# Trailing sums of the pooling branch on GpSimd; the subtractions stay on VectorE

## The chip, the core and the metric

The kernel runs on one core of one Trainium2 chip. The metric is the device time of one launch in microseconds (us). The kernel before took 1399.68 us in the median of 3 runs (1397.62 to 1403.03). All arithmetic is in 32-bit floats.

The engines are named as the profile names them: PE is TensorE (PEld its weight loads), DVE is VectorE, ACT is ScalarE, POOL is GpSimd, SP is SyncE. Each engine runs its own queue in program order. SP computes nothing here: it issues nearly all loads from memory, so its queue is the list of loads.

## The reference, cut to what matters

One decoder layer over 256 tokens of width 2048. A conditioning vector `c` gives shift, scale and gate vectors by a product with `w_ada` (2048 x 12288). The normed and modulated tokens go through one projection `w_in`, whose columns feed two branches: sparse attention (an indexer picks 64 keys per query) and the pooling branch. Both are joined by `w_out`; then follows a mixture of 32 experts. The pooling branch:

```python
cs = jnp.cumsum(pg, axis=1)
lag = cs_pad[:, lo, jnp.arange(POOL_GROUPS)[None, :], :]
count = jnp.minimum(t + 1, win[None, :]).astype(jnp.float32)
mixed = (cs - lag) / count[None, :, :, None] - pg
y = jnp.einsum('bsgc,gcd->bsgd', mixed.astype(p.dtype), w_pool) * pool_scale
```

There are 1024 pooling channels in 4 groups with windows 2, 4, 8 and 16: the mean over the last 2, 4, 8 or 16 tokens, minus the token itself, then one 256 x 256 matrix per group.

## The kernel before, in words

The channels lie on the 128 partitions and the 256 tokens along the free axis, so the pooled input `ppT` is 128 x 8 x 256 (two chunks of channels for each group). `pool_sums` (line 510) builds the sums by doubling: level 0 adds each token's neighbour (window 2) for all 8 chunks, level 1 adds the level before at a distance of 2 (window 4) for the last 6 chunks, then 4 and 2 chunks. The levels alternate between two buffers, `wa` and `wb`. On each level line 516 adds, line 517 copies the first tokens, which have no partner. Line 521 corrects the first 16 tokens of a group for the shorter window, and line 522 subtracts the token itself and writes back into `ppT`. `pool_map` (line 524) loads `w_pool` and does the matrices on PE (line 531).

What stands around it. The program is written against a scheduler that orders the instructions of each engine by priority and by its own estimates of time, so an edit on one engine can move instructions on all. The projection (`project`, line 458) runs in five blocks of rows of `w_in`; on the last block the indexer (line 362) and `pool_sums` come in between. PE writes projections into two PSUM banks called `mm`; line 470 on DVE adds a bank to `pidx` or `pqkv` and so frees it.

Fills: 64 slices of `w_ada` of 1 MB each (line 177 loads on SP, line 178 multiplies and adds on DVE, 128 x 2048 each) make gate 1, the second shift and scale, and gate 2. They are needed only later, and go in between other work. Their loads have three slots, first the two halves of G4 and one of G5, later G5's is replaced by B8 (shown as `w`). A slot is free for its next load when line 178 has read it. All sums go into an accumulator in G6. The last fill belongs to gate 2, which the first expert stage needs late (line 290).

After the projection: `out_proj` (line 602) for the pooling half and then for the attention half. Line 608 loads `w_out` in 16 pieces of 1 MB, line 613 is the product on PE, line 617 scales a PSUM bank by gate 1 and line 618 adds it to the residual, both on DVE. After each quarter of the attention half a routing block transposes and multiplies for the router (lines 679 to 697). The routing itself is a chain of small DVE instructions (lines 708 to 789). Then `gather` multiplies tokens into expert slots (line 796 on PE, line 800 on DVE), and the experts follow: line 815 and line 856 load 2 MB tiles of expert weights into a ring of seven 16 KB places (G5, G1, G2, G3, G0, G7, G4), line 820 and 861 multiply. Six of these loads stand in SP's queue before the number of tokens per expert is read (line 952), the seventh behind it; the seventh goes to G4, so it waits for the last fill's line 178.

In the order listings below, `g_70` is G4, `g_71` is G5 (the pooled input lies in its upper half), `g_72` is G6, and `g_68` and `g_69` are the places of `w_in` and `w_out`.

Of the kernel before, what the change touches and what calls it, by code (L numbers as in the profile page):

```python
# [16 lines left out]
P = 128  # L17
D = 2048
NT = 2
S = 256  # L20
# [27 lines left out]
EDGE = 16  # L48
# [31 lines left out]
def layer_kernel(ctx: ExitStack, tc: tile.TileContext, x, c, w_ada, b_ada, norm1_g, w_in, q_norm_g,  # L80
                 k_norm_g, w_pool, pool_scale, w_out, norm2_g, w_grp, w_exp, w1, w3, w2,
                 kconst, kband, out):
    nc = tc.nc
# [71 lines left out]
    for v, r, j, at in ((v8T, RB, 0, None), (v8T, RB, 1, 3), (v8T, RB, 2, 4), (v4T, RR, 0, None), (v4T, RR, 1, 4)):  # L155
        src = norm2_g[0] if at is None else b_ada[at * D:(at + 1) * D]
        nc.scalar.dma_start(v[:, j].rearrange("p k r -> p (k r)").rearrange("p (k r) -> p k r", r=r),
                            src.rearrange("(k p r) -> p k r", p=P, r=r))
    edge = one.tile([P, 4, EDGE], F32, name="edge")
# [104 lines left out]
    for kq in range(4):  # L264
# [5 lines left out]
        dst = hT[:, kq * 4:kq * 4 + 4]  # L270
# [239 lines left out]
    def pool_sums():  # L510
        wa = one.tile([P, 8, S], F32, tag="N0", name="wa")
        wb = one.tile([P, 8, S], F32, tag="N1", name="wb")
        src = ppT
        for lv, dst in enumerate((wa, wb, wa, wb)):
            c0, lag = 2 * lv, 1 << lv
            nc.vector.tensor_add(dst[:, c0:8, lag:S], src[:, c0:8, lag:S], src[:, c0:8, 0:S - lag])
            nc.vector.tensor_copy(dst[:, c0:8, 0:lag], src[:, c0:8, 0:lag])
            src = dst
        for g, dst in enumerate((wa, wb, wa, wb)):
            sl = slice(2 * g, 2 * g + 2)  # L520
            nc.vector.tensor_mul(dst[:, sl, 0:EDGE], dst[:, sl, 0:EDGE], edge[:, g][:, None, :].to_broadcast([P, 2, EDGE]))
            nc.vector.scalar_tensor_tensor(ppT[:, sl], dst[:, sl], 1.0 / POOL_WINDOWS[g], ppT[:, sl], op0=ALU.mult, op1=ALU.subtract)

    def pool_map():
# [14 lines left out]
    for b, (k0, nk) in enumerate(BLOCKS):  # L539
        block_scales(b)  # L540
        for k in range(k0, k0 + nk):
            h = hcols(k, slice(0, S))
            nc.scalar.activation(h, h, AF.Identity, scale=s1T[:, k:k + 1], bias=sh1T[:, k:k + 1])
        nxt = block_ada(b + 1) if b + 1 < len(BLOCKS) else []
        last = b + 1 == len(BLOCKS)
        for pi, part in enumerate(PARTS):
            if nxt:
                nxt.pop(0)()
            project(b, part)
            if pi == 2 and nxt:  # L550
                nxt.pop(0)()
            if last and part[0] == "kw":
                indexer()
                pool_sums()
            if b in FILLS:
                fill(FILLS[b][pi])
        for piece in nxt:
            piece()
# [427 lines left out]
```

## Time and profile before

| | |
|---|---|
| median of 3 runs | 1399.68 us |
| the profiled execution | 1398.5 us, span 1396.5 us |
| busy in the span: PE, DVE, ACT, POOL | 1071.1, 446.9, 100.1, 9.1 us |
| read from memory | 554.31 MB, 398 GB/s over the span |
| mean granted clock of PE | 0.888 |

The span is the stretch from the first to the last instruction of the profiled execution; 2 us lie around it. Times in a view count from the span's start. A line of a timeline has start, duration, engine, source line, operation, output and inputs, shapes, how many instructions were merged, and in brackets how long the engine was idle ahead of it and what ended that. `SPq` is SP's queue: its instructions only issue a load. The table of windows gives for each stretch how long each engine was busy, the granted clock of PE, the share of time in which the 16 DMA engines were busy, and the rate.

### The profile page before, as it was taken

How to read it: one execution, taken by the hardware profiler on the slowest of the kernel's cores; microseconds unless marked ns; L12 is line 12 of the kernel's file. 1: busy time of each engine (PE TensorE's matmuls, PEld its weight loads, DVE VectorE, ACT ScalarE, POOL GpSimd, SP SyncE). 2: the span in 40 equal slices, each digit the busy share in tenths (PEclk: the TensorE clock that was granted, in tenths of full speed). 3: DMA queues.
4: the chain of work that ended last, by engine and by line, in shares of the span. 5: the costliest groups of instructions: out<-in, count | busy, mean ns of one | idle time of the engine just before them, and what ended most of it. 6: DMA issues, size and time to landing. Idle time of an engine off the chain costs nothing.

```text
span 1396.5 us, 12529 instructions
## 1 busy us (share of the span) xinstructions
PE 1071.1 (77%) x5243; PEld 432.8 (31%) x5243; DVE 446.9 (32%) x725; ACT 100.1 (7%) x225; POOL 9.1 (1%) x11
## 2 busy tenths in 40 slices
PE   4899998998997776677758767676775867768566
PEld 2355654544456231122213213122211311312111
DVE  1196667999677210201202101020220202102002
ACT  3100000324222000000000000000000000000000
POOL 1000000000000000000000000000000000000000
PEclk9899999999997979889979988887997988898787
DMA  9999998999999799999999999999999999999997
GB/s 320 318 385 385 400 381 323 342 357 332 401 360 405 325 428 427 428 428 427 427 429 427 428 428 428 428 428 428 427 429 427 428 428 427 429 427 428 428 403 260
DMA packets 104907, 557.27 MB, mean 399 GB/s; under 512 B 18856, under 2 KB 33168, under 8 KB 72848
## 3 DMA queue, kind: packets, MB, share of 16 engines
q1 hardware_dynamic: 101312, 554.22, 97.8%
q10 hardware_dynamic: 3472, 2.20, 0.5%
q8 instruction: 43, 0.70, 0.2%
q14 instruction: 16, 0.13, 0.0%
q0 software_dynamic: 64, 0.02, 0.0%
HBM read 554.31 MB, written 2.10 MB: 398 GB/s over the span
## 4 chain that ended last, share of the span: by engine, by line
DMA 54%; PE 30%; DVE 8%; SPq 4%; issue 3%; ACT 1%; ACTq 0%; DVEq 0%
DMA w<-in_w_dram 49%; PE mm L820 10%; PE mm L613 5%; PE mm L475 5%; PE b L861 4%; DVE g L178 3%; DMA g<-in_w_ada_dram 3%; PE b L485 2%; DMA g<-in_w_in_dram 2%; SPq L876 1%; SPq L815 1%; DVE bacc L219 1%; PE b L796 1%; DVE g L408 1%; DMA v8T<-in_b_ada_dram 1%
## 5 line engine op out<-in xcount | busy, mean ns | idle before, releaser
L820 PE MATMUL mm<-w,xg 128*32 128x512 f32 x2048 | 338.0, 694 | 163.6 <-DMA w<-in_w_dram 163.6
L861 PE MATMUL b<-w,t 128*32 128x512 f32 x896 | 181.1, 697 | 86.4 <-DMA w<-in_w_dram 80.9
L820 PEld LDWEIGHTS mm<-w,xg 128*32 128x32 f32 x2048 | 76.3, 124 | 412.6 <-DMA w<-in_w_dram 231.0
L800 DVE TENSOR_SCALAR xg<-b,sc2T,sh2T 128x128 f32<-128x128 f32 x128 | 42.3, 403 | 386.4 <-PE b L796 386.4
L475 PE MATMUL mm<-g,hT 128*128 128x512 f32 (+1 forms) x320 | 127.9, 553 | 12.7 <-DMA g<-in_w_in_dram 7.8
L178 DVE SCALAR_TENSOR_TENSOR g<-g,sT,g 128x2048 f32<-128x2048 f32 x52 | 121.9, 2344 | 9.9 <-DMA g<-in_w_ada_dram 9.8
L613 PE MATMUL mm<-g,mix 128*128 128x512 f32 x256 | 114.7, 601 | 4.2 <-DVE t L617 4.2
L861 PEld LDWEIGHTS b<-w,t 128*32 128x32 f32 x896 | 42.3, 118 | 220.2 <-DMA w<-in_w_dram 118.6
L841 DVE TENSOR_TENSOR t<-b,gt 128x512 f32<-128x512 f32 (+1 forms) x33 | 20.9, 671 | 278.6 <-PE b L861 253.7
L475 PEld LDWEIGHTS mm<-g,hT 128*128 128x128 f32 x320 | 57.3, 199 | 79.1 <-issue 65.4
L613 PEld LDWEIGHTS mm<-g,mix 128*128 128x128 f32 x256 | 48.1, 193 | 60.7 <-issue 55.0
L844 PE MATMUL mm<-t,gwT 128*128 128x512 f32 (+1 forms) x132 | 63.6, 613 | 1.6 <-DVE t L841 1.1
L796 PEld LDWEIGHTS b<-gq,x1c 128*128 128x128 f32 x512 | 59.8, 196 | 13.1 <-issue 6.7
L796 PE MATMUL b<-gq,x1c 128*128 128x128 f32 x512 | 62.6, 282 | 1.2 <-DVE gq L786 1.2
L824 ACT ACTIVATE t<-mm 128x512 f32<-128x512 f32 x8 | 4.8, 597 | 816.8 <-PE mm L820 816.8
L485 PE MATMUL b<-hT,g 128*128 128x256 f32 x256 | 56.9, 380 | 0.9 <-DMA g<-in_w_in_dram 0.9
L485 PEld LDWEIGHTS b<-hT,g 128*128 128x128 f32 x256 | 48.3, 190 | 11.7 <-issue 3.3
L846 DVE TENSOR_TENSOR xs<-xs,mm 128x512 f32<-128x512 f32 (+1 forms) x66 | 44.3, 671 | 18.9 <-PE mm L844 18.7
L825 DVE TENSOR_TENSOR t<-t,mm 128x512 f32<-128x512 f32 x8 | 5.5, 688 | 117.5 <-PE mm L820 117.5
L219 DVE SCALAR_TENSOR_TENSOR bacc<-g,sT,bacc 128x1024 f32<-128x1024 f32 x28 | 35.9, 1282 | 7.6 <-DMA g<-in_w_ada_dram 5.1
L844 PEld LDWEIGHTS mm<-t,gwT 128*128 128x128 f32 x132 | 21.7, 192 | 43.5 <-DVE xs L846 28.4
L178 DVE SCALAR_TENSOR_TENSOR g<-w,sT,g 128x2048 f32<-128x2048 f32 x12 | 28.1, 2346 | 2.3 <-DMA w<-in_w_ada_dram 2.2
(208 smaller groups left out, 511.6 us busy)
## 6 DMA issues: line engine op xcount, KB each, us to landing
w<-in_w_dram SPq DMA_DIRECT2D x188, 2048.0 KB, 22.1
g<-in_w_ada_dram SPq DMA_DIRECT2D x52, 1024.0 KB, 8.2
g<-in_w_ada_dram SPq DMA_DIRECT2D x44, 512.0 KB, 9.4
g<-in_w_in_dram SPq DMA_DIRECT2D x21, 1024.0 KB, 10.3
g<-in_w_out_dram SPq DMA_DIRECT2D x16, 1024.0 KB, 9.6
w<-in_w_ada_dram SPq DMA_DIRECT2D x12, 1024.0 KB, 7.6
w<-in_w_ada_dram SPq DMA_DIRECT2D x20, 512.0 KB, 9.6
g<-in_w_in_dram SPq DMA_DIRECT2D x14, 512.0 KB, 8.7
```

What stands on the lines that cost most here:

```text
L178: nc.vector.scalar_tensor_tensor(acc, w, sT[:, k:k + 1], acc, op0=ALU.mult, op1=ALU.add)
L219: nc.vector.scalar_tensor_tensor(acc, w[:, kk], sT[:, k:k + 1], acc, op0=ALU.mult, op1=ALU.add)
L475: nc.tensor.matmul(po[:, :width], lhsT=hcols(k0 + j, slice(i * P, (i + 1) * P)), rhs=w[:, j], start=(j == 0), stop=(j == nk - 1))
L485: nc.tensor.matmul(ppool[n][:, u], lhsT=w[:, j, u * P:(u + 1) * P], rhs=hcols(k, slice(0, S)), start=(k == 0 and u % 2 == 0), stop=(k == K ...
L613: nc.tensor.matmul(po, lhsT=mix[:, k, i * P:(i + 1) * P], rhs=ws[k // 4][:, k % 4], start=(k == 0), stop=(k == 7))
L796: nc.tensor.matmul(px[:, u], lhsT=x1c[i][:, k // RB, k % RB], rhs=gq[:, i].rearrange("p e s -> p (e s)"), start=(i == 0), stop=(i == NT - 1))
L800: nc.vector.tensor_scalar(xg[:, k], px[:, u], sc2T[:, k:k + 1], sh2T[:, k:k + 1], op0=ALU.mult, op1=ALU.add)
L820: nc.tensor.matmul(h[e * CAP:(e + 1) * CAP, :], lhsT=xg[:, k, e * CAP:(e + 1) * CAP], rhs=ws[e][:, r], start=(k == 0), stop=(k == KC - 1), ...
L841: nc.vector.tensor_mul(y[:, 0:m], py, gt2[:, c0:c0 + m])
L844: nc.tensor.matmul(pz[:, 0:m], lhsT=gwT[:, i], rhs=y[:, 0:m], start=True, stop=True)
L846: nc.vector.tensor_add(xv, xv, pz[:, 0:m])
L861: nc.tensor.matmul(py[n // 2][e * CAP:(e + 1) * CAP, (n % 2) * 512:(n % 2 + 1) * 512], lhsT=aT[:, f, e * CAP:(e + 1) * CAP], rhs=ws[e][:, ...
```

## The change

The four additions, the four copies and the four corrections of the first tokens are issued on GpSimd in place of VectorE. Line 522 stays on VectorE.

```diff
@@ -513,12 +513,12 @@
         src = ppT
         for lv, dst in enumerate((wa, wb, wa, wb)):
             c0, lag = 2 * lv, 1 << lv
-            nc.vector.tensor_add(dst[:, c0:8, lag:S], src[:, c0:8, lag:S], src[:, c0:8, 0:S - lag])
-            nc.vector.tensor_copy(dst[:, c0:8, 0:lag], src[:, c0:8, 0:lag])
+            nc.gpsimd.tensor_add(dst[:, c0:8, lag:S], src[:, c0:8, lag:S], src[:, c0:8, 0:S - lag])
+            nc.gpsimd.tensor_copy(dst[:, c0:8, 0:lag], src[:, c0:8, 0:lag])
             src = dst
         for g, dst in enumerate((wa, wb, wa, wb)):
             sl = slice(2 * g, 2 * g + 2)
-            nc.vector.tensor_mul(dst[:, sl, 0:EDGE], dst[:, sl, 0:EDGE], edge[:, g][:, None, :].to_broadcast([P, 2, EDGE]))
+            nc.gpsimd.tensor_mul(dst[:, sl, 0:EDGE], dst[:, sl, 0:EDGE], edge[:, g][:, None, :].to_broadcast([P, 2, EDGE]))
             nc.vector.scalar_tensor_tensor(ppT[:, sl], dst[:, sl], 1.0 / POOL_WINDOWS[g], ppT[:, sl], op0=ALU.mult, op1=ALU.subtract)
```

GpSimd's queue gets the twelve instructions in one run, between the memset of line 366 and the third memset of line 281; the correction for a group stands right behind the copy of the level that it needs. Ahead of the first addition the build puts one instruction that reloads GpSimd's library; it waits for nothing.

DVE's queue at the pooling sums, before (`wa` and `wb` are the two buffers, `mm` a bank of the projection):

```order
L516 TENSOR_TENSOR wa<-g_71 128x8x255
L517 COPY wa<-g_71 128x8
L178 SCALAR_TENSOR_TENSOR g_72<-g_70,sT,g_72 128x2048
L516 TENSOR_TENSOR wb<-wa 128x6x254
L517 COPY wb<-wa 128x6x2
L521 TENSOR_TENSOR wa<-wa,edge 128x2x16
L470 TENSOR_TENSOR pidx<-pidx,mm 128x512
L178 SCALAR_TENSOR_TENSOR g_72<-g_70,sT,g_72 128x2048
L470 TENSOR_TENSOR pidx<-pidx,mm 128x512
L516 TENSOR_TENSOR wa<-wb 128x4x252
L517 COPY wa<-wb 128x4x4
L522 SCALAR_TENSOR_TENSOR g_71<-wa,g_71 128x512
```

The same place in the changed kernel, from the same point on:

```order
L178 SCALAR_TENSOR_TENSOR g_72<-g_70,sT,g_72 128x2048
L470 TENSOR_TENSOR pidx<-pidx,mm 128x512
L178 SCALAR_TENSOR_TENSOR g_72<-g_70,sT,g_72 128x2048
L470 TENSOR_TENSOR pidx<-pidx,mm 128x512
L178 SCALAR_TENSOR_TENSOR g_72<-g_71,sT,g_72 128x2048
L351 TENSOR_TENSOR g_73<-pidx,kc 128x64
L352 TENSOR_TENSOR g_73<-pidx,kc 128x64
L353 TENSOR_TENSOR g_73<-pidx,kc 128x64
L354 TENSOR_TENSOR g_73<-pidx,kc 128x64
L522 SCALAR_TENSOR_TENSOR g_71<-wa,g_71 128x512
L470 TENSOR_TENSOR pidx<-pidx,mm 128x512
L470 TENSOR_TENSOR pidx<-pidx,mm 128x80
```

The sums are gone, line 522 now waits for GpSimd, and the third line 470 stands behind it. Ahead of the last of the four lines 522 stand three lines 178, counted from here, where there were five.

SP's queue from the last load of `w_out` to the third load of expert weights, before:

```order
L608 DMA g_68<-in_w_out_dram 128x4x512
L177 DMA g_70<-in_w_ada_dram 128x2048
L177 DMA w<-in_w_ada_dram 128x2048
L177 DMA g_70<-in_w_ada_dram 128x2048 x2
L177 DMA w<-in_w_ada_dram 128x2048
L177 DMA g_70<-in_w_ada_dram 128x2048 x2
L177 DMA w<-in_w_ada_dram 128x2048
L815 DMA w<-in_w_dram 128x4096
```

And in the changed kernel:

```order
L608 DMA g_68<-in_w_out_dram 128x4x512
L177 DMA g_70<-in_w_ada_dram 128x2048 x2
L177 DMA w<-in_w_ada_dram 128x2048
L177 DMA g_70<-in_w_ada_dram 128x2048 x2
L177 DMA w<-in_w_ada_dram 128x2048
L177 DMA g_70<-in_w_ada_dram 128x2048 x2
L177 DMA w<-in_w_ada_dram 128x2048
L177 DMA g_70<-in_w_ada_dram 128x2048 x2
L177 DMA w<-in_w_ada_dram 128x2048
L177 DMA g_70<-in_w_ada_dram 128x2048 x2
L177 DMA w<-in_w_ada_dram 128x2048
L815 DMA w<-in_w_dram 128x4096
```

Eight fills stood there, now there are fifteen: four fewer stand ahead of the last `w_out` load (47 against 51), and three more ahead of this load of expert weights (62 against 59).

DVE's queue at the first gather, before:

```order
L786 TENSOR_SCALAR gq<-t_1899,rs_1857 128x128 x2
L789 TENSOR_TENSOR t_1899<-t_1899,cmb 128x256
L178 SCALAR_TENSOR_TENSOR g_72<-w,sT,g_72 128x2048
L178 SCALAR_TENSOR_TENSOR g_72<-g_70,sT,g_72 128x2048
L800 TENSOR_SCALAR xg<-b_1921,sc2T,sh2T 128x128 x8
L800 TENSOR_SCALAR xg<-b_1946,sc2T,sh2T 128x128 x8
L805 COPY gwT<-sm 128x256
L178 SCALAR_TENSOR_TENSOR g_72<-g_70,sT,g_72 128x2048
```

And in the changed kernel:

```order
L786 TENSOR_SCALAR gq<-t_1899,rs_1857 128x128 x2
L789 TENSOR_TENSOR t_1899<-t_1899,cmb 128x256
L178 SCALAR_TENSOR_TENSOR g_72<-g_70,sT,g_72 128x2048
L800 TENSOR_SCALAR xg<-b_1921,sc2T,sh2T 128x128 x8
L800 TENSOR_SCALAR xg<-b_1946,sc2T,sh2T 128x128 x8
L805 COPY gwT<-sm 128x256
```

The last fill moves from behind line 805 to ahead of the lines 800. In the routing ahead of this piece, the line 178 that stood between lines 731 and 732 is gone too, and the line 178 of the 63rd fill stands ahead of the last line 697.

## Rows read from the trace of the kernel before

**Rows 1.** The chain that ended last, by engine (the page, part 4).
```profile
DMA 54%; PE 30%; DVE 8%; SPq 4%; issue 3%; ACT 1%; ACTq 0%; DVEq 0%
```

**Rows 2.** Windows: start:end, length, busy us by engine, PEclk, DMA share, GB/s.
```profile
218.70:242.20 23.50, 19.89 (x63) 9.22 (x63) 23.41 (x39) 1.00 (x4) 0.00 (x0) 0.93 0.91 324
242.20:337.10 94.90, 89.01 (x329) 46.66 (x327) 91.27 (x180) 31.64 (x100) 4.11 (x3) 1.00 0.94 360
337.10:387.80 50.70, 49.95 (x133) 23.64 (x134) 38.69 (x35) 16.27 (x40) 0.00 (x0) 0.97 0.97 359
387.80:454.40 66.60, 56.94 (x263) 40.03 (x262) 50.95 (x79) 16.45 (x28) 0.00 (x0) 0.85 0.96 380
454.40:462.60 8.20, 8.20 (x79) 3.55 (x80) 7.25 (x17) 0.00 (x0) 0.00 (x0) 1.00 0.12 27
462.60:1381.00 918.40, 651.70 (x3646) 198.32 (x3636) 121.07 (x255) 8.40 (x13) 0.00 (x0) 0.86 1.01 425
```

**Rows 3.** Timeline of DVE at the pooling sums.
```profile
204.53 4.73 DVE L178 SCALAR_TENSOR_TENSOR g<-g,sT,g 128x2048 f32<-128x2048 f32 x2
218.79 2.28 DVE L516 TENSOR_TENSOR wa<-g 128x2040 f32<-128x2040 f32 x1 [9.52 <-ACT g L488]
...
233.32 0.68 DVE L470 TENSOR_TENSOR pidx<-pidx,mm 128x512 f32<-128x512 f32 x1
...
241.47 0.68 DVE L522 SCALAR_TENSOR_TENSOR g<-wb,g 128x512 f32<-128x512 f32 x1
```

**Rows 4.** Windows, line 516 alone: length, DVE busy, PEclk, DMA share, GB/s.
```profile
218.70:242.20 23.50, 5.88 (x4) 0.93 0.91 324
```

**Rows 5.** Groups of DVE instructions, 218 to 243: busy us, mean ns, idle.
```profile
L521 DVE TENSOR_TENSOR wa<-wa,edge 128x32 f32<-128x32 f32 x2 | 0.4, 180 | 0.0
...
L517 DVE COPY wb<-wa 128x12 f32<-128x12 f32 (+1 forms) x2 | 0.3, 165 | 0.0
```

**Rows 6.** Timeline of PE, 225 to 338.
```profile
225.89 4.55 PE L475 MATMUL mm<-g,hT 128*128 128x512 f32 x16
234.05 6.31 PE L475 MATMUL mm<-g,hT 128*128 128x80 f32 x16 [3.61 <-DVE pidx L470]
...
264.36 1.13 PE L531 MATMUL mm<-g,g 128*128 128x256 f32 x4
...
327.77 0.63 PE L593 MATMUL b<-kc,g 128*128 128x128 f32 x4 [1.78 <-DVE g L575]
329.07 1.13 PE L597 MATMUL sm<-spare,g 128*128 128x512 f32 x2 [0.68 <-ACT spare L594]
...
333.64 0.75 PE L307 MATMUL fl<-kc,t 128*128 128x128 f32 x4 [0.72 <-ACT t L304]
337.85 10.31 PE L613 MATMUL mm<-g,mix 128*128 128x512 f32 x20 [3.46 <-DVE t L617]
```

**Rows 7.** Timeline of SP's queue: loads issued.
```profile
384.33 3.81 SPq L608 DMA_DIRECT2D g<-in_w_out_dram  x2
...
461.13 4.73 SPq L815 DMA_DIRECT2D w<-in_w_dram  x5
```

**Rows 8.** Timeline of DVE, routing and first gather.
```profile
437.68 0.23 DVE L697 TENSOR_TENSOR lr<-lr,sm 128x72 f32<-128x72 f32 x1 [3.78 <-PE sm L686]
...
440.06 2.33 DVE L178 SCALAR_TENSOR_TENSOR g<-g,sT,g 128x2048 f32<-128x2048 f32 x1
...
452.52 2.64 DVE L800 TENSOR_SCALAR xg<-b,sc2T,sh2T 128x128 f32<-128x128 f32 x8 [0.31 <-PE b L796]
...
458.76 2.35 DVE L178 SCALAR_TENSOR_TENSOR g<-g,sT,g 128x2048 f32<-128x2048 f32 x1
```

**Rows 9.** Timeline of POOL, memsets.
```profile
174.26 0.53 POOL L366 MEMSET qiT<- 128x512 f32 x1 [140.96 <-PE sm L229]
260.41 1.82 POOL L281 MEMSET g<- 128x2048 f32 x1 [85.63 <-PE fl L290]
```

## Prediction

> **What bounds the kernel now.** I read the chain that ended last first: 54% of it is DMA and 30% PE, and only 8% is DVE [rows 1]. So an engine that gets lighter is worth nothing by itself; it has to let loads go out earlier. The table of windows says where that is possible. From 462.6 to 1381 the DMA engines are busy all the time at 425 GB/s [rows 2]: there the end follows the moment at which the stream of expert weights starts, and nothing else. Ahead of it the share is 0.91 to 0.97, with one real hole, 8.2 us at a share of 0.12 (454.4 to 462.6), ahead of the seventh load of expert weights [rows 2]. DVE is busy 23.41 of 23.50 us at the pooling sums and 91.27 of 94.90 us behind them, and PE is nearly full beside it [rows 2]. So in this part three resources are close to full together, and a gain on one soon meets the next.
>
> **What leaves DVE.** The four additions are 5.88 us [rows 4]; four corrections at 0.18 and four copies at 0.165 are 1.4 us [rows 5]. Together 7.3 us of DVE. They don't come off the time directly. The new order also lets DVE do a fill in the 9.52 us in which it waited for ACT ahead of the first addition [rows 3], but has three line 178 ahead of the last line 522, where five stood: 2 x 2.34 us are put off, not saved.
>
> **What GpSimd takes.** No row shows an addition on GpSimd. Its memsets take 1.82 us for 2048 and 0.53 for 512 elements [rows 9], so 0.84 ns for each element that is written and 0.10 us for each instruction. The additions have 2040 + 1524 + 1008 + 496 = 5068 elements, and there are twelve instructions. Lower bound, as if only the writing counted: 4.3 + 1.2 = 5.5 us. Upper bound, two reads and one write at that rate one after another: 12.8 + 1.2 = 14.0 us. I take the upper end, since an addition moves three such streams. What DVE waits for first is the correction of group 0, behind two additions and two copies: 3564 elements, 9.0 + 0.5 = 9.5 us from 218.8, so 228.3 (222.3 by the lower bound).
>
> [...]
>
> **Where DVE and PE meet.** PE stops at 230.44 (225.89 + 4.55) until 234.05, because line 470 frees a bank late, at 233.32, behind pooling work [rows 3, 6]. In the new order this line 470 stands behind the first line 522. DVE reaches that 522 so: the second line 470 starts when PE has its bank, at 225.9, and then 0.68 + 2.34 (the third fill) + four small instructions of about 0.18 = 229.6. GpSimd is done at 228.3, so its cost is hidden, with 1.3 us to spare. Then 0.68 for line 522 and 0.68 for line 470: PE goes on at 231.0 and not 234.05, a gain of 3.0 us. Further on PE is held up four times, 1.78 + 0.68 + 0.72 + 3.46 = 6.6 us [rows 6]. These waits can all go, as DVE has less to do ahead of them (three fills and the sums, 14.3 us), or stay, as PE comes 3 us earlier itself and DVE stops at four lines 522. I count a third, 2.2 us, since both engines are nearly full up to there. So PE, and with it the last load of `w_out` at 388 [rows 7], comes 5.2 us earlier; the bounds are 0 and 9.6. The rest is covered: `pool_map` starts at 264.36 [rows 6], some 30 us behind the last line 522, and the next memset on GpSimd at 260.41 [rows 9].
>
> **What the put-off fills cost.** Four fewer fills stand ahead of this last load of `w_out`. One is 1 MB (1.049 million bytes), at 380 GB/s 2.76 us [rows 2], so 11.0 us of transfers are moved into the stretch from 387.8 to 454.4, which has only 4% of 66.6 us = 2.7 us to give [rows 2]. Balance: transfers run 11.0 - 5.2 - 2.7 = 3.1 us late there. This meets the routing, because the 63rd fill now stands on DVE ahead of the last line 697. Behind that fill SP's queue has three expert tiles and one more fill, 7 MB, until the stage's transfers end at 454.4. At 2.76 us for each that is 435.1, at the 425 GB/s of the later stage 437.1; I take 436. With the 3.1 us and its line 178 (2.34) that is 441.4, and line 697 stood at 437.68 [rows 8]: 3.8 us later. In return the line 178 at 440.06, which held up the chain of the routing, is gone: 2.3 us. Routing ends 1.5 us later.
>
> **What the last fill gives back.** Before, the last fill ended at 458.76 + 2.35 = 461.11, behind the lines 800, and the seventh tile was issued at 461.13 [rows 7, 8]. Now it is done ahead of the lines 800 (452.52 [rows 8]), so about 454 with the delay, and one 2 MB tile goes into the hole: 2.097 MB at 425 GB/s = 4.9 us. More doesn't fit, since the next four wait for PE's first line 820. If the fill comes late, down to nothing is gained.
>
> **Sum.** 1.5 - 4.9 = -3.4 us. Against the profiled execution's 1398.5 us that is 1395.1; the median is 1.2 us above that execution, so I forecast 1399.68 - 3.4 = 1396.3 us.
>
> **Rivals.**
>
> *The two engines hold each other up.* If GpSimd can't work while DVE runs an instruction with two operands from SBUF, the fills and the chain of sums take turns: two line 178 and the small ones, 5.4 us, are added to 228.3. PE then goes on at 233.7 + 1.36 = 235.1, 1.0 us later than before, so PE's gain is 2.2 - 1.0 = 1.2, transfers are 7.1 us late, and the sum is 7.8 - 2.3 - 4.9 = +0.6: 1400.3 us. No row shows both engines at work on SBUF for long (a memset only writes), so the trace neither speaks for nor against it. [...]
>
> *The lighter DVE passes everything on.* All of PE's stops at 327 to 338 go: PE gains 9.6 us, transfers are 1.3 us ahead, line 697 comes 0.7 us earlier, and the sum is -0.7 - 2.3 - 4.9 = -7.9: 1391.8 us. For it: 14.3 us less DVE work ahead of line 617 at 337. Against: 89.01 of 94.90 us of PE are busy there anyway [rows 2].
>
> *GpSimd is far slower and DVE stands at line 522.* DVE's queue is in order; behind the first 522 stand the lines 470 that PE needs and the indexer's rope. Cover ends at 229.6; the change loses from 233.1 on (14.3 us for the first five instructions), and each further us is lost whole. If they take 24 us, 2.5 times my upper bound, PE goes on at 244.4, loses 8.1 us on balance, transfers are 16.4 us late, and the sum is 17.1 - 2.3 - 4.9 = +9.9: 1409.6 us. For it: no addition on GpSimd was ever timed here, and a library reload stands ahead of it. Against: the reload waits for nothing and has the 44 us from 174.8 to 218.8 [rows 3, 9].
>
> [...]
>
> **How the numbers follow.** Forecast 0.48 (its own range 1393 to 1400), exclusion 0.23, passed on 0.17, far slower 0.12. The range 1390 to 1405 takes in the first three and the near part of the last. 0.5% (7.0 us) is about what a measurement tells from no change. Faster than 1392.7: four fifths of "passed on" and a little of the forecast, 0.19. Slower than 1406.7: most of "far slower", 0.10. Within: 0.71.
>
> **What would show it.** Right: PE's stop at 230 is under 1 us; the additions on GpSimd sum to 9 to 14 us; the last load of `w_out` is issued at 381 to 385; the last line 697 stands at 437 to 443; the seventh expert tile is issued ahead of 456 and the hole is shorter by about 5 us. Wrong: DVE idle for more than 3 us ahead of a line 522, PE's stop at 230 longer than before, or a hole ahead of the experts as long as it was.

## The result and the profile after

| | before | after |
|---|---|---|
| median | 1400.75 us (6 runs beside it) | 1407.49 us (6 runs, 1406.49 to 1409.66) |
| the profiled execution's span | 1396.5 us | 1404.6 us |
| busy: PE, DVE, POOL | 1071.1, 446.9, 9.1 us | 1074.9, 446.7, 24.4 us |
| mean granted clock of PE | 0.888 | 0.884 |

The ratio is 1.0055 with a 95% interval of [1.0042, 1.0067]: 0.55% is 7.7 us (the two medians are 6.7 us apart). The forecast was 1396.3, the range 1390 to 1405; both were wrong. One line of the table already says much: 7.3 us of work left DVE, and DVE is as busy as before, 446.7 against 446.9 us. The rows at the pooling sums show why, POOL first (start, duration, engine, line, operation, tiles):

```profile
217.25 3.58 POOL L516 TENSOR_TENSOR wa<-g 128x2040 f32<-128x2040 f32 x1 [44.06 <-ACT g L488]
220.79 0.19 POOL L517 COPY wa<-g 128x8 f32<-128x8 f32 x1
221.06 2.73 POOL L516 TENSOR_TENSOR wb<-wa 128x1524 f32<-128x1524 f32 x1
223.73 2.26 POOL L517 COPY wb<-wa 128x12 f32<-128x12 f32 x1
225.94 0.25 POOL L521 TENSOR_TENSOR wa<-wa,edge 128x32 f32<-128x32 f32 x1
226.15 1.87 POOL L516 TENSOR_TENSOR wa<-wb 128x1008 f32<-128x1008 f32 x1
227.97 2.26 POOL L517 COPY wa<-wb 128x16 f32<-128x16 f32 x1
...
230.39 1.22 POOL L516 TENSOR_TENSOR wb<-wa 128x496 f32<-128x496 f32 x1
```

and DVE at the same place:

```profile
220.79 0.69 DVE L470 TENSOR_TENSOR pidx<-pidx,mm 128x512 f32<-128x512 f32 x1 [8.14 <-PE mm L475]
221.39 4.54 DVE L178 SCALAR_TENSOR_TENSOR g<-g,sT,g 128x2048 f32<-128x2048 f32 x1
...
226.45 3.72 DVE L178 SCALAR_TENSOR_TENSOR g<-g,sT,g 128x2048 f32<-128x2048 f32 x1
...
230.44 1.26 DVE L353 TENSOR_TENSOR g<-pidx,kc 128x64 f32<-128x64 f32 x1
...
231.76 0.75 DVE L522 SCALAR_TENSOR_TENSOR g<-wa,g 128x512 f32<-128x512 f32 x1
```

Read the ends together. The fill that starts at 221.39 takes 4.54 us where a fill takes 2.33 to 2.35 [rows 8]: the addition on POOL ends at 223.79, and 2.14 us later, nearly a whole fill, comes the fill's end, 225.93. POOL's copy of 12 elements stands from 223.73 to 225.99, over that same fill; copies of 8 and 16 elements with no fill beside them take 0.19 us (at 220.79 and 231.56). Then an addition runs to 228.02, and the next fill, begun at 226.45, ends at 230.17, again 2.15 us behind it, and the copy of 227.97 ends with the fill. So here, of two such instructions, one runs and the other waits for its end. Line 470, which reads one operand from PSUM, takes no part: 0.69 us beside the addition of 221.06, and that addition is not held up. Stretched by this are the two fills and line 353 (1.26 us, 0.21 before), together 2.20 + 1.38 + 1.05 = 4.6 us of DVE. That is most of the 7.3 us; where the rest of DVE's busy time comes from was not followed.

PE's stop at 230 [rows 6] is still there, and it is longer:

```profile
224.26 4.55 PE L475 MATMUL mm<-g,hT 128*128 128x512 f32 x16
233.16 6.85 PE L475 MATMUL mm<-g,hT 128*128 128x80 f32 x16 [4.35 <-DVE pidx L470]
...
398.01 1.94 PE L301 MATMUL fl<-g,ones 128*32 128x512 f32 x8 [10.88 <-DVE g L178]
```

The pooled input is there when line 488 ends on ACT, at 217.17, before at 218.75 (the row after, then the row before):

```profile
216.16 1.01 ACT L488 COPY g<-b 128x1024 f32<-128x1024 f32 x1 [5.89 <-PE b L485]
```

```profile
217.74 1.01 ACT L488 COPY g<-b 128x1024 f32<-128x1024 f32 x1 [5.89 <-PE b L485]
```

So this execution ran 1.6 us ahead of the kernel before up to here. Counted from that moment, PE goes on after 15.99 us, before after 15.30; the forecast was 12.25. Of the later stops, those at 327 to 338 shrank as forecast (6.6 to 4.25 us over four), and a new one of 10.88 us stands at 387 to 398 (called the stop at 388 below): line 301 waits for a fill on DVE, which waits for its load. The table of windows, with the bounds of [rows 2] (length, busy of PE, PEld, DVE, ACT and POOL with their counts, granted clock, DMA share, GB/s):

```profile
218.70:242.20 23.50, 19.15 (x60) 9.39 (x59) 20.75 (x36) 0.65 (x2) 13.84 (x12) 0.85 0.89 334
...
387.80:454.40 66.60, 50.10 (x190) 31.20 (x190) 54.33 (x74) 15.86 (x27) 0.00 (x0) 0.76 0.97 382
454.40:462.60 8.20, 7.91 (x49) 7.91 (x50) 4.57 (x9) 0.00 (x0) 0.00 (x0) 0.68 1.00 402
462.60:480.00 17.40, 15.01 (x97) 5.36 (x95) 5.41 (x17) 2.35 (x4) 0.00 (x0) 1.00 0.47 182
```

The hole ahead of the experts has moved from 454.4 into the last row (share 0.47); it has not gone. At the routing and the gather, DVE's rows that answer to [rows 8]:

```profile
447.55 0.23 DVE L697 TENSOR_TENSOR lr<-lr,sm 128x72 f32<-128x72 f32 x1 [0.74 <-PE sm L686]
...
455.21 2.35 DVE L178 SCALAR_TENSOR_TENSOR g<-g,sT,g 128x2048 f32<-128x2048 f32 x1
461.16 2.64 DVE L800 TENSOR_SCALAR xg<-b,sc2T,sh2T 128x128 f32<-128x128 f32 x8 [3.60 <-PE b L796]
```

and SP's that answer to [rows 7]:

```profile
380.34 3.81 SPq L608 DMA_DIRECT2D g<-in_w_out_dram  x2
...
447.54 26.89 SPq L815 DMA_DIRECT2D w<-in_w_dram  x6
```

The last loads of `w_out` go out 4.0 us earlier than before (1.6 us of this is the head start), yet the last line 697 stands at 447.55, 9.9 us later. So the time is lost in two places: some of it before 242, and most of it is visible only behind 388. In the chain that ended last DMA keeps its 54%, and PE rises from 30% to 36% [rows 1].

```profile
DMA 54%; PE 36%; DVE 5%; SPq 2%; issue 2%; ACT 1%; ACTq 0%; DVEq 0%
```

### The profile page after: what moved, and what is told of

It is laid out like the page before. It is cut to its first block, busy times and chain, and to the rows that moved or that the text cites. A ratio compares the mean times of both kernels' runs of the same rounds, so it can differ in the third digit from the quotient of the medians.

```text
span 1404.6 us, 12545 instructions
## 1 busy us (share of the span) xinstructions
PE 1074.9 (77%) x5243; PEld 435.6 (31%) x5243; DVE 446.7 (32%) x713; ACT 100.5 (7%) x225; POOL 24.4 (2%) x23
## 4 chain that ended last, share of the span: by engine, by line
DMA 54%; PE 36%; DVE 5%; SPq 2%; issue 2%; ACT 1%; ACTq 0%; DVEq 0%
DMA w<-in_w_dram 50%; PE mm L820 10%; PE mm L475 6%; PE mm L613 6%; PE b L861 4%; PE b L485 4%; DVE g L178 2%; DMA g<-in_w_in_dram 2%; DMA g<-in_w_ada_dram 2%; SPq L815 1%; PE mm L498 1%; DVE bacc L219 1%; PE b L796 1%; DMA v8T<-in_b_ada_dram 1%; PE mm L531 1%
## 5 line engine op out<-in xcount | busy, mean ns | idle before, releaser
L178 DVE SCALAR_TENSOR_TENSOR g<-g,sT,g 128x2048 f32<-128x2048 f32 x52 | 125.5, 2413 | 15.8 <-DMA g<-in_w_ada_dram 15.5
L881 PE MATMUL b<-w,t 128*32 128x512 f32 (+1 forms) x160 | 19.2, 590 | 12.2 <-DMA w<-in_w_dram 11.5
```

Of the source, the lines that this page charges most:

```text
L178: nc.vector.scalar_tensor_tensor(acc, w, sT[:, k:k + 1], acc, op0=ALU.mult, op1=ALU.add)
```

## The experiments

Three theories were open. *Turns*: GpSimd and DVE exclude each other, so the work is not hidden. *Order*: the new order of the queues costs the time, whatever engine does the sums. *Put-off fills*: one part of the order does it, the fills that now stand later (the stop of 10.88 us). In most experiments each engine's queue is given its order by a list, called from line 952, which waits for nothing and leaves the line numbers as they are. "Order of before" and "order of after" are such lists. Every time stands beside the kernel before on the same chip. The times are medians; the ratio is an estimate from all runs of both, with its 95% interval, and can lie 0.1% off the quotient of the medians. Rows come from one execution of each kernel.

### The two parts of the change apart

The sums on GpSimd with every queue in the order of before; and the sums on VectorE with the order of after:

```diff
-            nc.vector.tensor_add(dst[:, c0:8, lag:S], src[:, c0:8, lag:S], src[:, c0:8, 0:S - lag])
+            nc.gpsimd.tensor_add(dst[:, c0:8, lag:S], src[:, c0:8, lag:S], src[:, c0:8, 0:S - lag])
...
+    in_order(nc, tc); rv = nc.values_load(mosti[0:1, 0:1], min_val=0, max_val=S)
```

> The twelve instructions of the sums run on GpSimd as in the changed kernel, but every engine's queue has the order of the kernel before (VectorE's without the twelve). Theory 'order': the loss lies in the order of the queues, not in what GpSimd takes, so this is near the kernel before, 1397 to 1402 us, and TensorE has no stop of 10 us at 387. Theory 'price': GpSimd's additions and the stretched VectorE instructions beside them cost it, so this is near the changed kernel, 1405 to 1409 us.

Measured: 1403.49 against 1402.02 us, 1.0011 [0.9999, 1.0023]. Here too the engines take turns, and line 522 is hit as well (2.12 us for 0.68, behind a POOL addition):

```profile
220.51 4.53 DVE L178 SCALAR_TENSOR_TENSOR g<-g,sT,g 128x2048 f32<-128x2048 f32 x1
225.56 2.12 DVE L522 SCALAR_TENSOR_TENSOR g<-wa,g 128x512 f32<-128x512 f32 x1
```

> The sums run on VectorE as in the kernel before, but TensorE, ScalarE and SyncE have the order of the changed kernel, and VectorE too, with the twelve instructions put in behind the ones that they followed before. Theory 'order': about as slow as the changed kernel, 1405 to 1410 us, with the stop of TensorE ahead of line 301 at about 387, 9 us or longer. Theory 'price': near the kernel before, 1399 to 1402 us.

Measured: 1405.88 against 1402.02 us, 1.0030 [1.0018, 1.0042]; the stop at 388 is 9.86 us, with no GpSimd in it. So the order alone costs 0.3%, and GpSimd in place of VectorE 0.11% in the one order (its interval just takes in no change), 0.25% in the other. Neither theory has it all.

### No sums at all, in both orders

Both kernels leave the sums out: line 522 reads the pooled input alone.

```diff
-            nc.vector.scalar_tensor_tensor(ppT[:, sl], dst[:, sl], 1.0 / POOL_WINDOWS[g], ppT[:, sl], op0=ALU.mult, op1=ALU.subtract)
+            nc.vector.scalar_tensor_tensor(ppT[:, sl], ppT[:, sl], 1.0 / POOL_WINDOWS[g], ppT[:, sl], op0=ALU.mult, op1=ALU.subtract)
```

> The sums are left out on both engines (line 522 reads the pooled input itself), with every queue in the order of the changed kernel, so it times the changed order without any price of GpSimd. Theory 'order': within 2 us of the changed kernel, 1405 to 1409 us, with the stop at 387. Theory 'price': 4 to 7 us less than the changed kernel, 1400 to 1403 us, and no line 178 over 2.5 us at 221 to 230.

Measured: 1399.83 against 1402.02 us, 0.9995 [0.9983, 1.0007]. This is what the forecast described, a change whose sums cost nothing. DVE's fills take their usual time, and PE hardly stops:

```profile
222.78 2.35 DVE L178 SCALAR_TENSOR_TENSOR g<-g,sT,g 128x2048 f32<-128x2048 f32 x1
...
441.30 0.23 DVE L697 TENSOR_TENSOR lr<-lr,sm 128x72 f32<-128x72 f32 x1 [0.74 <-PE sm L686]
```

```profile
230.50 4.59 PE L475 MATMUL mm<-g,hT 128*128 128x80 f32 x16 [0.30 <-DVE pidx L470]
391.84 1.93 PE L301 MATMUL fl<-g,ones 128*32 128x512 f32 x8 [9.62 <-DVE g L178]
```

PE goes on 11.95 us behind the pooled input (forecast 12.25), and the last line 697 stands at 441.30 (forecast 441.4). The nearness of the second is partly luck, as the memsets below show. The stop at 388 is there all the same, in a kernel that is as fast as the one before; so that stop is no cause by itself.

> The sums left out on both engines (line 522 reads the pooled input itself), every queue in the order of the kernel before. Beside the kernel before it prices the 7.3 us of VectorE work in that order, and beside the kernel without sums in the changed order it compares the two orders with no sums in them. Theory 'the changed order is worse in itself': 1393 to 1397 us, as 5 us are gained by leaving the sums out here too. Theory 'the orders are equal, the sums cost': 1398 to 1401 us, no more than 2 us from the kernel without sums in the changed order.

Measured: 1396.67 against 1400.35 us, 0.9968 [0.9955, 0.9981]. The whole removal of the 7.3 us is worth 4.5 us in the old order, and this is the most that any move to another engine could have brought there. The order costs 0.27% without sums (0.9968 to 0.9995, give or take 0.18% by the two intervals), 0.30% with them on VectorE and 0.44% on GpSimd.

### GpSimd works, and nobody waits for it

To tell a wait for GpSimd from its mere presence: the twelve instructions stay, in the order of after, but line 522 reads the pooled input (the edit above), so their result goes nowhere.

> The order of the changed kernel, GpSimd does the twelve instructions, but line 522 reads the pooled input in their place, so nothing waits for GpSimd. Beside the kernel without any sums in the same order it prices the work of GpSimd beside VectorE without the wait. Theory 'exclusion': the two line 178 at 221 and 226 stay at 3.7 to 4.5 us, and it is as slow as the changed kernel within 2 us, 1405 to 1408 us. Theory 'wait': without the wait at line 522 it is as fast as the kernel without sums, 1399 to 1402 us.

Measured: 1407.69 against 1400.81 us, 1.0045 [1.0029, 1.0062]. On DVE and on PE:

```profile
223.82 4.53 DVE L178 SCALAR_TENSOR_TENSOR g<-g,sT,g 128x2048 f32<-128x2048 f32 x1
```

```profile
235.58 6.27 PE L475 MATMUL mm<-g,hT 128*128 128x80 f32 x16 [4.34 <-DVE pidx L470]
```

The fills are as long as in the changed kernel, and PE goes on 15.99 us behind the pooled input, to the hundredth. Not one wait for GpSimd's result is in it. Against the kernel without sums in the same order PE starts 4.04 us later, and then its 16 matmuls take 6.27 us and not 4.59. The windows over them (no sums first, then this kernel) show the granted clock at 1.00 behind a stop of 0.30 us and at 0.73 behind one of 4.34 us:

```profile
230.50:235.10 4.60, 4.60 (x18) 2.64 (x19) 4.60 (x15) 0.00 (x0) 0.00 (x0) 1.00 1.02 390
```

```profile
235.60:241.90 6.30, 6.30 (x18) 3.53 (x19) 6.17 (x22) 0.00 (x0) 0.00 (x0) 0.73 0.97 336
```

4.04 + 1.68 = 5.7 us behind at 242. In the time it is 0.50% = 7.0 us (give or take 2.9). At the last line 697, counted from the pooled input, it is 7.0 us too, but there single executions differ by several us, as the next kernel shows.

Then GpSimd with work of the same length that only writes: no sums, and one copy and seven memsets of 2048 elements (12.9 us) where the twelve were.

```diff
+        nc.gpsimd.tensor_copy(wa[:, :, 0:1], ppT[:, :, 0:1])
+        for n in range(7):
+            nc.gpsimd.memset((wa, wb)[n % 2], 0.0)
```

> The order of the changed kernel, no sums (line 522 reads the pooled input itself), and on GpSimd in the place of the twelve instructions one small copy that starts when the first addition did, and seven memsets of 128x2048, 12.9 us in all, nearly the 13.8 us of the sums. They write SBUF and read nothing. Theory 'exclusion by reads': the fills beside them stay at 2.35 us, TensorE goes on at 230.5, and the time is that of the kernel without sums, 1398 to 1402 us. Rival 'any work of GpSimd slows VectorE': as the kernel with the twelve instructions unused, 1405 to 1409 us.

Measured: 1400.66 against 1400.35 us, 1.0000 [0.9989, 1.0011]. GpSimd busy with memsets costs nothing that can be measured here: POOL is at its memsets, the fill beside them takes its 2.35 us, and PE goes on after 11.95 us.

```profile
222.85 1.81 POOL L515 MEMSET wa<- 128x2048 f32 x1
```

```profile
223.28 2.35 DVE L178 SCALAR_TENSOR_TENSOR g<-g,sT,g 128x2048 f32<-128x2048 f32 x1
```

In this execution the stop at 388 is 12.69 us, not 9.62, and the last line 697 stands at 446.58, not 441.30, though the order is the same and no sums are done in either. The times of all runs show no such difference (1.0000 and 0.9995), so up to 5 us at line 697 belong to the single execution.

The last of this row: the unused sums again, with two of the fills as a multiplication by one tensor operand (they leave out the addition to what was there).

```diff
-            nc.vector.scalar_tensor_tensor(acc, w, sT[:, k:k + 1], acc, op0=ALU.mult, op1=ALU.add)
+            (nc.vector.tensor_scalar(acc, w, sT[:, k:k + 1], None, op0=ALU.mult) if sec == 2 and k in (13, 14) else nc.vector.scalar_tensor_tensor(acc, w, sT[:, k:k + 1], acc, op0=ALU.mult, op1=ALU.add))
```

> The kernel with the changed order in which GpSimd does the twelve instructions and nothing waits for them, with one more edit: the two fills that stand beside GpSimd's additions (the 14th and 15th of the first section) are a multiplication by a number for each partition with one operand from SBUF, in place of multiply-and-add with two, so gate 1 is not what it should be. Theory 'two operands exclude': these fills take no more than they would alone, GpSimd's copies of 128x12 and 128x16 stay at 0.2 us and its chain is 3 to 4 us shorter, TensorE goes on about 12 us after the pooled input is there (as without sums) and not 16, and the time is 1399 to 1403 us. Rival 'any VectorE instruction excludes': GpSimd's copies are still stretched by the length of a fill, and the time is 1404 to 1408 us.

Measured: 1404.59 against 1400.32 us, 1.0028 [1.0016, 1.0041], between the two forecasts. DVE and POOL:

```profile
221.40 3.47 DVE L178 TENSOR_SCALAR g<-g,sT 128x2048 f32<-128x2048 f32 x1
```

```profile
223.73 1.19 POOL L517 COPY wb<-wa 128x12 f32<-128x12 f32 x1
```

The form still takes turns: the fill waits for the addition's end at 223.79 and is done 1.08 us later, where the usual fill needed 2.14, and the copy waits as long. PE goes on 13.86 us behind the pooled input. So neither theory holds as it stood: one operand did not free the engines, but it halved what each turn costs. Why this form needs half as long, and still takes turns, no run shows.

### Less on GpSimd

Only the first addition and its copy on GpSimd, in the order of before:

```diff
-            nc.vector.tensor_add(dst[:, c0:8, lag:S], src[:, c0:8, lag:S], src[:, c0:8, 0:S - lag])
+            (nc.vector if lv else nc.gpsimd).tensor_add(dst[:, c0:8, lag:S], src[:, c0:8, lag:S], src[:, c0:8, 0:S - lag])
```

> The kernel before with only the first addition and its copy on GpSimd, every queue in the order of the kernel before. VectorE waits 9.52 us for ScalarE ahead of this addition, so GpSimd works while VectorE has nothing to do, and the fill behind it is done in that wait. Theory 'exclusion': nothing stands beside VectorE work, the fills stay at 2.35 us, VectorE is 2 to 4 us ahead at the second addition, TensorE's stop at 230 shrinks from 3.6 to under 2 us, 1397 to 1400 us where the kernel before has 1401. Rival 'relief is worth nothing here': 1400 to 1402 us.

Measured: 1400.98 against 1400.35 us, 1.0002 [0.9991, 1.0013]. No turns are taken here, because DVE has nothing to do and waits; the wait was for ACT before [rows 3] and is for GpSimd now. PE's stop is 2.93 us (3.61 before, under 2 expected), and nothing comes of it at the end: the rival had it right.

```profile
223.07 1.75 DVE L516 TENSOR_TENSOR wb<-wa 128x1524 f32<-128x1524 f32 x1 [8.00 <-POOL wa L517]
```

### The stop at 388 and the put-off fills

First the stop itself: in the changed kernel line 301 goes behind three more groups of line 613, and lines 617 ahead of the fills.

```
 L686 MATMUL sm<-ws_1558,g_73 128x36 x8
+L613 MATMUL mm<-g_68,mix 128x512 x4
+L613 MATMUL mm<-g_69,mix 128x512 x4
+L613 MATMUL mm<-g_68,mix 128x512 x4
 L301 MATMUL fl<-g_72,ones 32x512 x4
```

> The changed kernel with its order, but for one place: line 301 for the second shift stands behind twelve more instructions of line 613 on TensorE, and on VectorE the two lines 617 that free both banks stand ahead of the 47th to 49th fill. The loads keep their order. Theory 'order': the stop of 10.9 us at 387 shrinks below 4 us and 6 to 10 us come back, 1397 to 1402 us. Rival 'transfers': the four fills that come behind the last w_out load make the routing late whatever TensorE does, 1405 us or more. Rival 'price': 1405 us or more as well, and a late start at 233 is carried on.

Measured: 1412.09 against 1402.02 us, 1.0084 [1.0064, 1.0104]. The stop is gone, PE works on at 389, and the last line 697 is later than ever, at 452.38. The fills, now behind the lines 617, hold up earlier lines 697 and 618 on DVE, and PE waits for these.

```profile
389.33 12.21 PE L613 MATMUL mm<-g,mix 128*128 128x512 f32 x24 [1.47 <-DVE t L617]
```

```profile
428.40 0.61 PE L686 MATMUL sm<-ws,g 128*128 128x36 f32 x4 [3.55 <-DVE lr L697]
434.11 1.13 PE L679 MATMUL b<-kc,xs 128*128 128x128 f32 x4 [5.10 <-DVE xs L618]
```

```profile
452.38 0.23 DVE L697 TENSOR_TENSOR lr<-lr,sm 128x72 f32<-128x72 f32 x1 [0.74 <-PE sm L686]
```

Then the put-off fills: two of them earlier again, on DVE and with their loads on SP, once in the changed kernel and once without the sums.

```
 L178 SCALAR_TENSOR_TENSOR g_72<-g_71,sT,g_72 128x2048
+L178 SCALAR_TENSOR_TENSOR g_72<-g_70,sT,g_72 128x2048
 L351 TENSOR_TENSOR g_73<-pidx,kc 128x64
...
 L522 SCALAR_TENSOR_TENSOR g_71<-wb,g_71 128x512
+L178 SCALAR_TENSOR_TENSOR g_72<-g_70,sT,g_72 128x2048
```

> The changed kernel with its order, except that two fills are done earlier: on VectorE one more line 178 stands ahead of the first line 351 behind the third line 470, one more behind the second line 522; on SyncE one more fill is loaded ahead of w_pool and one more ahead of the first w_out load of the pooling half. All later fills move up by two, until two places drop out at the last w_out load, so 49 fills stand ahead of it and not 47. Theory 'starved loads': the fills put off behind the lines 522 leave the DMA engines idle at 242 to 260 (share 0.76 where the kernel before has 0.99), 2 MB are missing from there on, and TensorE's stop at 387 and the late routing follow from them. So the share at 242 to 260 is above 0.88, the stop at 387 is under 4 us, the last line 697 stands 4 to 8 us earlier, and the time is 1399 to 1403 us. Rival 'price of GpSimd': 1406 to 1409 us. Rival 'overloaded VectorE': two more fills delay TensorE by 2 x 2.35 us at 233 and what is won is lost again, 1405 to 1410 us.

Measured: 1406.21 against 1400.81 us, 1.0037 [1.0024, 1.0051]. The last line 697 stands at 448.11, no earlier than in the changed kernel.

> No sums, the changed order, and two fills moved to the front again as in the run that did so with the sums on GpSimd. Theory 'put-off fills': the 3.8 us (0.27%) between the two orders without sums come from the fills that the changed order puts off, so at least half of them come back, 1396 to 1398 us. Rival 'the rest of the order' (line 301 and the lines 617 behind the 48th fill's load, the last fills ahead of the last line 697): 1399 to 1401 us, with a stop ahead of line 301 of 5 us or more.

Measured: 1401.14 against 1400.32 us, 1.0007 [0.9995, 1.0018]. PE in the first, then in the second:

```profile
235.40 7.57 PE L475 MATMUL mm<-g,hT 128*128 128x80 f32 x16 [6.74 <-DVE pidx L470]
393.82 1.07 PE L301 MATMUL fl<-g,ones 128*32 128x512 f32 x8 [0.73 <-DVE g L178]
```

```profile
231.95 6.28 PE L475 MATMUL mm<-g,hT 128*128 128x80 f32 x16 [2.69 <-DVE pidx L470]
388.51 1.06 PE L301 MATMUL fl<-g,ones 128*32 128x512 f32 x8 [0.73 <-DVE g L178]
```

The stop at 388 shrinks to 0.73 us in both, and in both PE stands 2.4 us longer at 230 for it. Without sums nothing came back (0.9995 and 1.0007, the intervals overlap). With them the ratio went from 1.0055 to 1.0037, and these intervals overlap as well, so a small return isn't ruled out there. The theory of the put-off fills falls: it wanted half of the 3.8 us back without sums, and the fills cost about the same early as late.

### The two gains at the end

Both in the kernel before: line 178 taken out of the routing (one fill goes behind the lines 800 instead); and the last fill ahead of the lines 800.

```
 L731 MAX m_1876<-lm 128x8 x2
-L178 SCALAR_TENSOR_TENSOR g_72<-g_70,sT,g_72 128x2048
 L732 COPY l_1877<-m_1876 128x16
```

> The kernel before with one edit of VectorE's order: the line 178 that stands between lines 731 and 732 stands behind line 789, and one of the two that stood there goes behind the lines 800. By the prediction's step 2.3 us are gained, 1398 to 1400 us where the kernel before has 1402. Rival: the two gathers or the loads end last there anyway, no difference, 1401 to 1403 us.

Measured: 1402.06 against 1400.81 us, 1.0003 [0.9992, 1.0014]. From line 697 to line 796 it is 7.15 us and not 9.28, as forecast. But line 796 itself then takes 10.23 us, 8.87 before (first this kernel, then the one before):

```profile
446.78 10.23 PE L796 MATMUL b<-gq,x1c 128*128 128x128 f32 x64 [1.20 <-DVE gq L786]
```

```profile
446.96 8.87 PE L796 MATMUL b<-gq,x1c 128*128 128x128 f32 x64 [1.20 <-DVE gq L786]
```

The granted clock from 440.0 to 454.4 is 0.56 here and 0.65 before.

> The kernel before with one edit of VectorE's order: the last line 178 stands ahead of the lines 800 in place of behind line 805. By the prediction's step the seventh expert tile is issued some 5 us earlier, the hole is filled and 4.9 us are gained, 1396 to 1398 us. Rival 'TensorE opens the stream': the next four tiles wait for TensorE's first line 820, which the put-in fill delays by up to 2.3 us; the tile is issued earlier but 0 to 2 us are gained, 1400 to 1403 us.

Measured: 1401.27 against 1400.81 us, 1.0003 [0.9991, 1.0014]. The fill waits for its load, and everything behind it with it:

```profile
456.60 2.35 DVE L178 SCALAR_TENSOR_TENSOR g<-g,sT,g 128x2048 f32<-128x2048 f32 x1 [3.13 <-DMA g<-in_w_ada_dram]
```

```profile
459.33 7.94 PE L820 MATMUL mm<-w,xg 128*32 128x512 f32 x68 [1.67 <-DVE xg L800]
```

This execution reaches the last line 697 at 438.93, before at 437.68, so times are best counted from there. The seventh tile goes out after 20.1 us instead of 23.5, but PE's first line 820 starts after 20.4 instead of 18.3, and the next four tiles, which wait for it, go out after 28.3 instead of 26.2. That is what the rival said. Neither of the two gives anything by itself: a gain above 1.3 us lies outside both intervals.

## Why the prediction was wrong

The forecast was a change of -3.4 us, measured is +7.7 (0.55%), 11.1 us apart. Two steps failed.

**The step that failed: "GpSimd is done at 228.3, so its cost is hidden, with 1.3 us to spare".** The time on GpSimd was right: the correction of group 0 is done 9.0 us behind the pooled input (9.5 forecast), and the additions sum to 9.4 us (range 9 to 14). What was wrong is that work on GpSimd leaves DVE free. DVE reaches the first line 522 14.6 us behind the pooled input, not 10.8, and it has not waited there: its own fills were longer. Shown by the unused sums (same stretch with no wait) and by the memsets (busy GpSimd, no stretch, no cost). Its price in this order: 0.9995 without sums, 1.0055 in the changed kernel, 0.60% or 8.4 us (give or take 2.4), of which the unused work alone makes 7.0. The forecast had put this price at nothing.

The rival on exclusion named the mechanism, and its delay was right: PE at 235.1 and not 231.0, 4.1 us, measured 4.0 (15.99 against 11.95). But it carried this delay to the end as it was, 4.0 us (+0.6 against -3.4), where 8.4 were measured. The lower clock behind the stop (0.73 for 1.00) adds 1.7 by 242; where the rest comes from no run isolates. The second failed step is in its sum as well, so it gave +0.6 us for the whole and not +7.7. The kernel before has such a stop too (PE goes on after 15.3 us, at a granted clock of 0.71 from 234.05 to 240); the change kept the stop and took on the new order's costs. The rival's chance, 0.23, was also too low for a mechanism that no row spoke against.

**The second: "What the last fill gives back", 4.9 us, with the 2.3 us of the routing.** From the last line 697 to the end of the span it was 958.8 us before, 957.1 after and 956.0 without the sums: 1.8 to 2.8 us came back, not 7.2. These are single executions, so the size is rough. Of the 2.3 us only 0.4 is left at PE's first line 820, which starts 17.9 us behind the last line 697 and 18.3 before: line 796 takes 9.77 us (granted clock 0.74) and not 8.87 (0.83), and two matmuls of line 290 now stand ahead of line 820. The seventh tile did go out early, at 457.59 (461.13 before), but it is not what the stream waits for: the tiles behind it need line 820.

```profile
465.48 4.93 PE L820 MATMUL mm<-w,xg 128*32 128x512 f32 x44
```

```profile
455.98 7.94 PE L820 MATMUL mm<-w,xg 128*32 128x512 f32 x68
```

The first of these rows is the changed kernel's, the second is from before. So in the changed kernel the hole is still there, at 462.6 to 470:

```profile
462.60:470.00 7.40, 7.40 (x65) 3.57 (x67) 5.41 (x17) 0.59 (x1) 0.00 (x0) 1.00 0.22 92
```

Without sums the time is 0.7 us below that before (from 2.4 below to 1.0 above, by the interval), by the forecast 3.4, so everything but the exclusion misses 2.7. With its 8.4 that is the 11.1, by construction. The single executions miss more behind line 697, 4.4 to 5.4 us; what makes up for it isn't shown.

**What held.** 7.3 us left DVE's list; the last load of `w_out` went out at 383.8 (381 to 385 forecast), 1.6 us of it by the head start; the line 178 left the routing, and line 732 follows line 731 at once (449.73 and 450.05); PE's stops at 327 to 338 gave back 2.4 us (2.2 forecast). Without the sums the last line 697 stands 3.6 us later than before (3.8 forecast), but executions of one order differ by more than that here, so this is no proof. "PE's stop at 230 longer than before" and a hole as long as it was were named as signs of error, and so they came. One slip in the working changes nothing: in the rival of the far slower GpSimd, 218.8 + 24 + 0.68 + 0.68 is 244.2 and not 244.4.

**What stays open.** Where the order of after loses 3.8 us against the order of before when there are no sums (0.9968 to 0.9995): with the fills late PE stops at 388, with two of them early it stops at 230, and the time is the same. That DVE and PE are both nearly full up to 337, so that a fill stops one or the other wherever it stands, fits with this, but no run isolates it. Whether all the sums on GpSimd would pay beside instructions that don't exclude it wasn't tried; the first level, beside an idle DVE, brought nothing (1.0002). No version here that does the sums beats the kernel before.

## What to carry to other kernels

Before work goes from DVE to GpSimd, list what DVE will run in those microseconds. Here it was fills that read two tensors from SBUF: they took turns with GpSimd's additions (4.54 us beside one, 2.35 alone), and 7.3 us taken off DVE came back as 4.6 us of waiting there. Price a stop of PE at more than its length where the granted clock behind it is lower: one that was 4.0 us longer stood here at 5.7 us once the matmuls behind it had run, at a granted clock of 0.73 in place of 1.00. And a transfer that starts earlier can be worth nothing: with the last fill early the seventh tile went out 3.4 us earlier, the four behind it 2.1 us later, and the time stayed the same (1.0003).

## What the runs showed of the hardware

In the changed kernel the turns were whole instructions, whichever came first: a copy of 12 elements on GpSimd stood for 2.26 us where copies of 8 and 16 with no fill beside them took 0.19, and a fill for 4.54 us where it takes 2.35. The memsets of 1.81 us took no part (2.35 us for the fill beside them), nor did line 470 with its one operand in PSUM (0.67 to 0.69 us). Additions on GpSimd took 3.58, 2.73, 1.87 and 1.22 us for 2040, 1524, 1008 and 496 elements, 1.5 ns for each element more; on DVE 2040 took 2.28 us [rows 3] and 496 took 0.66 us.
